# Both parts of an activation in one 512-wide product, and the farthest tap of the feed-forward convolution on ScalarE

## The chip, the cores and the metric

The kernel runs on one core of a Trainium2 chip. The metric is the time of one execution on the device in microseconds; the time shown is the median of three runs. TensorE (PE) multiplies matrices, VectorE (DVE) and ScalarE (ACT) work elementwise, each engine takes its instructions in the order in which they are written for it, and an instruction may have to wait for semaphores that other engines raise. PE writes its sums to PSUM; everything else lies in SBUF.

## The reference, cut to what matters

Two layers over x of 256 positions by 1024 channels. A layer is a norm, a projection into three mixers (SSD, retention, gated linear attention), their merge and a residual add; then a norm and a feed-forward part with a causal convolution of three taps over positions, and a residual add. A last norm ends it. All in float32.

```python
def conv_ffn(h, w_up, conv_w, conv_b, w_down):
    u = causal_dwconv(h @ w_up, conv_w, conv_b)      # 1024 -> 2 x 2816 channels, 3 taps
    gate, val = jnp.split(u, 2, axis=-1)
    return (jax.nn.silu(gate) * val) @ w_down        # 2816 -> 1024
...
    xbc = jax.nn.silu(causal_dwconv(xbc, ssm_conv_w, ssm_conv_b))   # 768 channels, 4 taps
...
for i in range(DEPTH):
    h = rms_norm(x, norm_mix_g[i])
    x = x + hybrid_mixer(h, w_in[i], ...)
    h = rms_norm(x, norm_ffn_g[i])
    x = x + conv_ffn(h, w_up[i], ffn_conv_w[i], ffn_conv_b[i], w_down[i])
return rms_norm(x, norm_f_g)
```

## The kernel before

Each float32 product is made from three products of a rounded type (fp32r). An operand is split into a high part and a low part (what the rounding left): high times high, high times low, low times high are added up in PSUM. The weights come from HBM in pieces of 128x1024 (tile raw). ACT casts a piece to its high part (whi, L183) and DVE subtracts that to get the low part (wlo, L184): each piece costs one such cast and one such subtraction, in the order in which the pieces are used. The activations are split once per norm into the tiles slot_h and slot_l (L302 on ACT, L303 on DVE).

There are two forms of product. In the form tok (tok_major, L274 to L276) the activations are the stationary operand and the weights stream 512 wide; a result takes two PSUM banks. In the form chan (chan_steps, L227 to L229) the weights are stationary and the activations stream, 256 positions wide, so that the result has channels on the partitions, as the convolutions need them. One chan result holds two channel blocks of 128 side by side in one PSUM bank (128x512) and takes 16 groups of three products: 8 steps k over the 1024 input channels for each of the two blocks j. A layer has 9 chan results in its mixers (xbc 3, rq 2, rk 2, gq 1, gk 1) and 22 in its feed-forward part (up), 62 in all.

The scale of the norm is not in the operands: it is applied when a result leaves PSUM, by a multiply with r_bc, the factors of the 256 positions on all partitions. DVE works them out (a chain of small steps that ends with dg, L319), PE spreads them (L322) and ACT copies them out of PSUM (L324). Until then no result can be drained.

PSUM has eight banks: four for the tag mm, which the chan and tok results share, and four for the tag mx.

The start of a mixer: xbc blocks 2 and 0 are made at once, in steps that alternate (chan_two, by the list LATE = (0, 2, 8, 10, 4, 12, 6, 14), in which 0 to 6 are block 2 and 8 to 14 block 0); then xbc block 1, then a narrow result (narrow, L256 and L260, one bank, drained by L475 into the tile small), then z in the form tok. Each xbc result goes through take_xbc: multiply by r_bc (L459), two activations for the nearest tap and the bias (L463), six steps for the other taps on DVE (L466), a tanh (L470), a last step (L471).

The feed-forward part alternates: block j of up (16 chan groups) and the down products of an earlier block (12 products 512 wide, L1024 to L1026, in mx). activate() drains an up block: multiply by r_bc (L1007), two activations (L1012), four steps for the two other taps (L1014), silu (L1016), gate times value (L1017), and the split into high and low part (L1018 on ACT, L1019 on DVE). Layer 0's down is followed by the residual adds (L365) and by layer 1's start.

The order on each engine is fixed when the program is built, by a scheduler that goes over what the generators yield.

## Time and profile before

| | |
|---|---|
| median of 3 runs | 933.4 us (932.29 to 935.02) |
| the profiled execution | 932.3 us, its span 930.5 us |
| mean granted clock of PE | 0.994 |
| busy: PE / weight loads | 914.5 / 816.1 us |
| busy: DVE / ACT / POOL | 712.9 / 506.8 / 78.4 us |
| HBM read | 165.81 MB, 179 GB/s over the span |

A busy time is the sum of an engine's instructions as the profiler saw them. Instructions on PE overlap, so the length of one is more than the time from its start to the next one's start; it is that distance that tells what a product costs. The granted clock is that of PE, as a share of its full 2.4 GHz.

### The profile page before, as it was taken

The page shows a single profiled execution, that of the slowest core. Times are in us where ns is not written, and L with a number is a line of the kernel's source. Part 1 is how long each engine was busy: PE and PEld are TensorE (multiplying, and loading weights), DVE is VectorE, ACT ScalarE, POOL GpSimd, SP SyncE. Part 2 cuts the span into 40 slices and gives each one's busy share as a digit, 9 for nine tenths or more (in the row PEclk, how much of TensorE's full clock was granted, in tenths as well). Part 3 has the DMA queues.
Part 4 walks back from the last instruction along what each step waited for, and adds up shares of the span by engine and source line. Part 5 has one row for each costly group of instructions (what it writes and reads, how often), then busy time and mean ns, then how long its engine had stood idle before and what let it go on. Part 6 is the DMA issues. An engine that isn't in the chain of part 4 may idle for free.

```text
span 930.5 us, 14996 instructions
## 1 busy us (share of the span) xinstructions
PE 914.5 (98%) x5726; PEld 816.1 (88%) x5726; DVE 712.9 (77%) x1111; ACT 506.8 (54%) x748; POOL 78.4 (8%) x74
## 2 busy tenths in 40 slices
PE   8999999999999999999999999999999999999995
PEld 7879889888889999999898898888888999999994
DVE  6976888576768887787799578777667697777775
ACT  6765454454456555555566635554545575555552
POOL 3032200003200000000002131000120000000001
PEclk9999999999999999999999999999999999999998
DMA  7775655556655656555466556444665566555531
GB/s 255 276 243 166 219 172 170 152 162 210 201 181 161 202 183 186 188 192 181 147 186 183 198 168 218 158 139 156 206 212 194 169 188 189 190 183 184 183 109 46
DMA packets 51288, 169.94 MB, mean 183 GB/s; under 512 B 5968, under 2 KB 8336, under 8 KB 51088
## 3 DMA queue, kind: packets, MB, share of 16 engines
q1 hardware_dynamic: 50928, 168.46, 56.3%
q8 instruction: 45, 0.74, 0.3%
q10 hardware_dynamic: 288, 0.52, 0.2%
q14 instruction: 27, 0.22, 0.1%
HBM read 165.81 MB, written 1.05 MB: 179 GB/s over the span
## 4 chain that ended last, share of the span: by engine, by line
PE 94%; DVE 3%; ACT 1%; DMA 1%; issue 0%; SPq 0%; ACTq 0%
PE mm L227 13%; PE mm L228 13%; PE mm L229 13%; PE mm L274 12%; PE mm L275 12%; PE mm L276 12%; PE mx L1025 4%; PE mx L1024 4%; PE mx L1026 4%; PE mx L555 2%; DVE wlo L184 1%; PE mx L558 1%; DVE xbc L466 1%; PE mx L542 1%; DMA x_t<-x_t 1%; PE mx L726 1%
## 5 line engine op out<-in xcount | busy, mean ns | idle before, releaser
L184 DVE TENSOR_TENSOR wlo<-raw,whi 128x1024 fp32r<-128x1024 f32 (+1 forms) x300 | 377.6, 1261 | 123.6 <-ACT whi L183 120.6
L183 ACT CAST whi<-raw 128x1024 fp32r<-128x1024 f32 (+1 forms) x302 | 311.7, 1034 | 266.4 <-PE mm L276 109.3
L227 PE MATMUL mm<-slot_h,whi 128*128 128x256 f32 x992 | 282.4, 285 | 2.2 <-ACT slot_h L302 2.2
L228 PE MATMUL mm<-slot_l,whi 128*128 128x256 f32 x992 | 281.5, 284 | 0.1
L229 PE MATMUL mm<-slot_h,wlo 128*128 128x256 f32 x992 | 281.5, 284 | 0.0
L274 PE MATMUL mm<-whi,slot_h 128*128 128x512 f32 x512 | 203.9, 398 | 0.0
L275 PE MATMUL mm<-wlo,slot_h 128*128 128x512 f32 x512 | 200.4, 391 | 0.0
L276 PE MATMUL mm<-whi,slot_l 128*128 128x512 f32 x512 | 200.3, 391 | 0.0
L227 PEld LDWEIGHTS mm<-slot_h,whi 128*128 128x128 f32 x992 | 190.5, 192 | 4.9 <-ACT slot_h L302 2.6
L228 PEld LDWEIGHTS mm<-slot_l,whi 128*128 128x128 f32 x992 | 190.7, 192 | 2.1 <-DVE slot_l L303 0.3
L229 PEld LDWEIGHTS mm<-slot_h,wlo 128*128 128x128 f32 x992 | 190.7, 192 | 0.1
L274 PEld LDWEIGHTS mm<-whi,slot_h 128*128 128x128 f32 x512 | 96.2, 188 | 20.6 <-issue 0.7
L276 PEld LDWEIGHTS mm<-whi,slot_l 128*128 128x128 f32 x512 | 96.1, 188 | 20.3
L275 PEld LDWEIGHTS mm<-wlo,slot_h 128*128 128x128 f32 x512 | 96.3, 188 | 18.7
L1014 DVE SCALAR_TENSOR_TENSOR tm<-tm,par 128x255 f32<-128x255 f32 (+1 forms) x176 | 73.6, 478 | 0.7 <-ACT tm L1012 0.7
L1024 PE MATMUL mx<-whi,slot_h 128*128 128x512 f32 x176 | 69.1, 392 | 0.0
L1025 PE MATMUL mx<-wlo,slot_h 128*128 128x512 f32 x176 | 69.0, 392 | 0.0
L1026 PE MATMUL mx<-whi,slot_l 128*128 128x512 f32 x176 | 68.5, 389 | 0.0
L1012 ACT ACTIVATE tm<-tm,par 128x256 f32<-128x256 f32 x88 | 48.0, 592 | 4.3 <-DVE tm L1007 4.3
L1007 DVE TENSOR_TENSOR tm<-mm,r_bc 128x512 f32<-128x512 f32 x44 | 30.4, 690 | 23.1 <-PE mm L229 23.1
L1018 ACT CAST slot_h<-tm 128x256 fp32r<-128x256 f32 x44 | 17.9, 406 | 49.1 <-DVE tm L1017 49.0
L1026 PEld LDWEIGHTS mx<-whi,slot_l 128*128 128x128 f32 x176 | 33.1, 188 | 7.1
(193 smaller groups left out, 758.6 us busy)
## 6 DMA issues: line engine op xcount, KB each, us to landing
raw<-w_all SPq DMA_DIRECT2D x292, 512.0 KB, 3.5
gate_b<-gate_b SPq DMA_DIRECT2D x12, 256.0 KB, 3.5
st<-ret_decay SPq DMA_DIRECT2D x8, 384.0 KB, 3.8
raw<-w_all SPq DMA_DIRECT2D x10, 256.0 KB, 3.9
x_t<-x_t SPq DMA_DIRECT2D x4, 256.0 KB, 5.8
xt<-x_tok SPq DMA_DIRECT2D x1, 1024.0 KB, 6.3
r_c<-q SPq DMA_DIRECT2D x16, 64.0 KB, 2.0
r_d<-q SPq DMA_DIRECT2D x16, 64.0 KB, 2.0
```

What stands on the lines that cost most here:

```text
L183: nc.scalar.copy(h_out, r_in)
L184: nc.vector.tensor_tensor(l_out, r_in, h_out.bitcast(F32), ALU.subtract)
L227: nc.tensor.matmul(o, lhsT=wh[:, c], rhs=ah[:, k, :], start=first, stop=False)
L228: nc.tensor.matmul(o, lhsT=wh[:, c], rhs=al[:, k, :], start=False, stop=False)
L229: nc.tensor.matmul(o, lhsT=wl[:, c], rhs=ah[:, k, :], start=False, stop=last)
L274: nc.tensor.matmul(acc[t], lhsT=ah[:, k, c], rhs=wh, start=first, stop=False)
L275: nc.tensor.matmul(acc[t], lhsT=ah[:, k, c], rhs=wl, start=False, stop=False)
L276: nc.tensor.matmul(acc[t], lhsT=al[:, k, c], rhs=wh, start=False, stop=last)
L1014: nc.vector.scalar_tensor_tensor(a[:, d:], u[:, :T - d], mx.pc("fconv_w", 3 * ct + 2 - d), a[:, d:], ALU.mult, ALU.add)
L1024: nc.tensor.matmul(o, lhsT=ah[:, a, tok], rhs=wh, start=first, stop=False)
L1025: nc.tensor.matmul(o, lhsT=ah[:, a, tok], rhs=wl, start=False, stop=False)
L1026: nc.tensor.matmul(o, lhsT=al[:, a, tok], rhs=wh, start=False, stop=last)
```

## The change

The high and the low part of an activation now lie side by side in one tile (both, 128 x n x 2 x 256). In a chan group the high part of the weights is multiplied with both at once, 512 wide, and the low part of the weights with the high part, 256 wide, into the first half. A chan result is then two halves that have to be added: it takes two PSUM banks (a pair), and a new function joined() copies the second half out on ACT and adds the first to it on DVE, into an SBUF tile. The multiply by r_bc works in place on that tile. The four banks of mm become two pairs; a tok result takes one pair, as its two banks did; narrow takes a pair and uses half of one bank.

In the feed-forward convolution the farthest tap of each of the two channel blocks becomes an ACT activation into a tile far, and one DVE add of 128x2x254 adds it for both; two of the four steps on DVE go.

```diff
--- before.py
+++ after.py
@@ -156,9 +156,8 @@
 
     slots = []
     for i, n in enumerate((KT, KT, 4)):
-        h = cpool.tile([P, n, T], F32R, name=f"slot_h{i}")
-        lo = cpool.tile([P, n, T], F32R, name=f"slot_l{i}")
-        slots.append((h, lo))
+        both = cpool.tile([P, n, 2, T], F32R, name=f"slot{i}")
+        slots.append((both[:, :, 0, :], both[:, :, 1, :], both))
 
 
     loaded = {}
@@ -193,7 +192,7 @@
         return (a[:, c] for a in piece(p + o // step))
 
     def mm_tile():
-        return ps.tile([P, 512], F32, name="mm", tag="mm", bufs=4)
+        return ps.tile([P, 2, 512], F32, name="mm", tag="mm", bufs=2)
 
     def mx_tile():
         return ps.tile([P, 512], F32, name="mx", tag="mx", bufs=4)
@@ -214,27 +213,31 @@
         return r_bc.unsqueeze(1).to_broadcast([P, 2, T])
 
 
-    def chan_steps(l, kind, idx, act, acc, ks, nk=KT, cols=256, width=256, col0=0):
-
-        ah, al = act
-        nj = width // P
+    def chan_steps(l, kind, idx, act, acc, ks, nk=KT):
+
+
+        ah, _, both = act
         for k in ks:
-            wh, wl = weight(l, kind, idx, k, cols)
-            for j in range(nj):
-                c = slice(col0 + j * P, col0 + (j + 1) * P)
-                o = acc[:, j * T:(j + 1) * T]
-                first, last = k == 0 and j == 0, k == nk - 1 and j == nj - 1
-                nc.tensor.matmul(o, lhsT=wh[:, c], rhs=ah[:, k, :], start=first, stop=False)
-                nc.tensor.matmul(o, lhsT=wh[:, c], rhs=al[:, k, :], start=False, stop=False)
-                nc.tensor.matmul(o, lhsT=wl[:, c], rhs=ah[:, k, :], start=False, stop=last)
-
-    def chan_major(l, kind, idx, act, nk=KT, **more):
+            wh, wl = weight(l, kind, idx, k, 256)
+            for j in range(2):
+                c = slice(j * P, (j + 1) * P)
+                nc.tensor.matmul(acc[:, j, :], lhsT=wh[:, c], rhs=both[:, k], start=(k == 0), stop=False)
+                nc.tensor.matmul(acc[:, j, :T], lhsT=wl[:, c], rhs=ah[:, k, :], start=False, stop=(k == nk - 1))
+
+    def joined(acc):
+
+        u = t_main()
+        nc.scalar.copy(two(u), acc[:, :, T:])
+        nc.vector.tensor_tensor(two(u), acc[:, :, :T], two(u), ALU.add)
+        return u
+
+    def chan_major(l, kind, idx, act, nk=KT):
         acc = mm_tile()
         for k in range(0, nk, 2):
-            chan_steps(l, kind, idx, act, acc, (k, k + 1), nk, **more)
+            chan_steps(l, kind, idx, act, acc, (k, k + 1), nk)
             if k < nk - 2:
                 yield
-        return acc
+        return joined(acc)
 
     def chan_two(l, kind, idx, act, take):
 
@@ -243,13 +246,13 @@
             i, k = n // 8, n % 8
             chan_steps(l, kind, idx[i], act, acc[i], (k, k + 1))
             if k == KT - 2:
-                take(idx[i], acc[i])
+                take(idx[i], joined(acc[i]))
             yield
 
     def narrow(l, act):
 
-        ah, al = act
-        acc = mm_tile()
+        ah, al, _ = act
+        acc = mm_tile()[:, 0, :]
         both = piece(PIECE_AT[l, "small", 0][0])[0].rearrange("p (k c) -> p k c", c=P)
         for k in range(KT):
             def low():
@@ -264,8 +267,9 @@
 
     def tok_major(l, kind, act, chunk=0, nk=KT):
 
-        ah, al = act
-        acc = [mm_tile() for _ in range(2)]
+        ah, al, _ = act
+        pair = mm_tile()
+        acc = [pair[:, t, :] for t in range(2)]
         for k in range(nk):
             wh, wl = weight(l, kind, chunk + k // 4, k % 4, 512)
             for t in range(2):
@@ -444,8 +448,7 @@
             nc.gpsimd.memset(self.wa, 0.0)
             for o in (32, 96):
                 nc.sync.dma_start(self.wa[o:o + 16, :], wa2[l])
-            y_h, y_l = slots[1]
-            self.y_dst = [(y_h[:, 0:4, :], y_l[:, 0:4, :]), (y_h[:, 4:8, :], y_l[:, 4:8, :]), slots[2]]
+            self.y_dst = [tuple(a[:, o:o + 4] for a in slots[1]) for o in (0, 4)] + [slots[2]]
 
         def pc(self, name, i=0, n=1):
             return self.pr[:, PO[name] + i:PO[name] + i + n]
@@ -455,7 +458,7 @@
             half = self.half
             if not hasattr(self, "xbc"):
                 self.xbc = mix.tile([P, 6, T], F32, name="xbc", tag="g_work")
-            ub = t_main()
+            ub = acc
             nc.vector.tensor_tensor(two(ub), two(acc), bc2(self.norm.r_bc), ALU.mult)
             for j in range(2):
                 ct = 2 * b + j
...
@@ -999,20 +1002,22 @@
 
 
         fx = slots[1]
-        ah, al = slots[2]
+        ah, al, _ = slots[2]
         dacc = []
 
         def activate(j, acc):
-            ub = t_main()
+            ub = acc
             nc.vector.tensor_tensor(two(ub), two(acc), bc2(norm.r_bc), ALU.mult)
             cv = t_main()
+            far = tmp.tile([P, 512], F32, name="far", tag="gt", bufs=4)
             for i in range(2):
                 ct = j + NF * i
-                u, a = ub[:, i * T:(i + 1) * T], cv[:, i * T:(i + 1) * T]
+                u, a, f = (q[:, i * T:(i + 1) * T] for q in (ub, cv, far))
                 nc.scalar.activation(a, u, AF.Identity, scale=mx.pc("fconv_w", 3 * ct + 2), bias=mx.pc("fconv_b", ct))
-                for d in (1, 2):
-                    nc.vector.scalar_tensor_tensor(a[:, d:], u[:, :T - d], mx.pc("fconv_w", 3 * ct + 2 - d),
-                                                   a[:, d:], ALU.mult, ALU.add)
+                nc.scalar.activation(f, u, AF.Copy, scale=mx.pc("fconv_w", 3 * ct))
+                nc.vector.scalar_tensor_tensor(a[:, 1:], u[:, :T - 1], mx.pc("fconv_w", 3 * ct + 1), a[:, 1:],
+                                               ALU.mult, ALU.add)
+            nc.vector.tensor_tensor(two(cv)[:, :, 2:], two(cv)[:, :, 2:], two(far)[:, :, :T - 2], ALU.add)
             nc.scalar.activation(cv[:, :T], cv[:, :T], AF.Silu)
             nc.vector.tensor_tensor(cv[:, :T], cv[:, :T], cv[:, T:], ALU.mult)
             nc.scalar.copy(ah[:, j % 4, :], cv[:, :T])
```

The part left out gives operands of the same shapes their new layout. What the change does to the order shows at three places. First PE at the start of layer 0's mixer, from the end of xbc block 1 (mm_378 before, mm_347 now) through narrow (L260 before, L263 now) to z (L274 before, L278 now). Before:

```order
L227 MATMUL mm_378<-slot_h0_87,whi_228 128x256
L228 MATMUL mm_378<-slot_l0_88,whi_228 128x256
L229 MATMUL mm_378<-slot_h0_87,wlo_229 128x256
L260 MATMUL mm_452<-slot_h0_87,whi_246 128x256 [waits Activation_49]
L256 MATMUL mm_452<-slot_l0_88,whi_246 64x256
...
L274 MATMUL mm_477<-whi_278,slot_h0_87 128x512
L275 MATMUL mm_477<-wlo_279,slot_h0_87 128x512
```

And of the change:

```order
L326 MATMUL mx_301<-dg_298,ones_79 128x256 [waits DVE_49]
L225 MATMUL mm_347<-slot0_87,wlo_218 128x256
L224 MATMUL mm_347<-slot0_87,whi_217 128x512
L225 MATMUL mm_347<-slot0_87,wlo_218 128x256
L263 MATMUL mm_407<-slot0_87,whi_231 128x256 [waits DVE_49,PE_49]
L259 MATMUL mm_407<-slot0_87,whi_231 64x256
...
L278 MATMUL mm_432<-whi_255,slot0_87 128x512 [waits DVE_49]
L279 MATMUL mm_432<-wlo_256,slot0_87 128x512
```

A group is two products in place of three. The first products of narrow and of z now wait for DVE: by the semaphores' values, narrow for the join of xbc block 0 (tm_332), z for the multiply into small.

Second, DVE at the same start, from dg to small. Before (tm_334 and tm_365 are xbc blocks 2 and 0):

```order
L319 TENSOR_SCALAR dg_326<-cs_76,rs_y_311 128x128
L184 TENSOR_TENSOR wlo_279<-raw_277,whi_278 128x1024 [waits DMAHW4_49,Activation_49]
L459 TENSOR_TENSOR tm_334<-mm_168,r_bc_331 128x512 [waits Activation_49]
L184 TENSOR_TENSOR wlo_349<-raw_347,whi_348 128x1024 [waits DMAHW5_49,Activation_49]
...
L184 TENSOR_TENSOR wlo_381<-raw_379,whi_380 128x1024 [waits DMAHW7_49,Activation_49]
L471 SCALAR_TENSOR_TENSOR xbc_333<-tm_344,xbc_333 128x512 [waits Activation_49]
L459 TENSOR_TENSOR tm_365<-mm_169,r_bc_331 128x512 [waits PE_49]
...
L475 TENSOR_TENSOR small_475<-mm_452,r_bc_331 128x256 [waits PE_49]
```

Of the change (tm_276 and tm_332 are the same two blocks, and L231 is the join):

```order
L231 TENSOR_TENSOR tm_276<-mm_165,tm_276 128x512 [waits Activation_49]
...
L183 TENSOR_TENSOR wlo_256<-raw_254,whi_255 128x1024 [waits DMAHW4_49,Activation_49]
...
L323 TENSOR_SCALAR dg_298<-cs_76,rs_y_283 128x128
L183 TENSOR_TENSOR wlo_320<-raw_318,whi_319 128x1024 [waits DMAHW5_49,Activation_49]
L462 TENSOR_TENSOR tm_276<-tm_276,r_bc_303 128x512 [waits Activation_49]
L183 TENSOR_TENSOR wlo_350<-raw_348,whi_349 128x1024 [waits DMAHW7_49,Activation_49]
...
L474 SCALAR_TENSOR_TENSOR xbc_305<-tm_315,xbc_305 128x512 [waits Activation_49]
L231 TENSOR_TENSOR tm_332<-mm_166,tm_332 128x512 [waits Activation_49]
L183 TENSOR_TENSOR wlo_410<-raw_408,whi_409 128x1024 [waits DMAHW1_49,PE_49]
L462 TENSOR_TENSOR tm_332<-tm_332,r_bc_303 128x512 [waits DVE_49]
...
L478 TENSOR_TENSOR small_430<-mm_407,r_bc_303 128x256 [waits PE_49]
```

The join of block 2 and one more wlo stand ahead of dg. The join of block 0 stands behind the whole convolution of block 2, and small behind the multiply, the join and five of the six steps of block 0 (one after the other in the rows left out, with a multiply of r_a between).

Third, DVE in the feed-forward part, one block in the steady state. Before:

```order
L1007 TENSOR_TENSOR tm_8458<-mm_8397,r_bc_7439 128x512 [waits PE_49]
L184 TENSOR_TENSOR wlo_8473<-raw_8471,whi_8472 128x1024 [waits DMAHW7_49,Activation_49]
L1014 SCALAR_TENSOR_TENSOR tm_8460<-tm_8458,par1_75,tm_8460 128x255 [waits Activation_49] x2
```

Of the change:

```order
L231 TENSOR_TENSOR tm_8233<-mm_8188,tm_8233 128x512 [waits Activation_49]
L1010 TENSOR_TENSOR tm_8233<-tm_8233,r_bc_6870 128x512 [waits DVE_49]
L183 TENSOR_TENSOR wlo_8271<-raw_8269,whi_8270 128x1024 [waits DMAHW2_49,Activation_49]
L1018 SCALAR_TENSOR_TENSOR tm_8237<-tm_8233,par1_75,tm_8237 128x255 [waits Activation_49] x2
L1020 TENSOR_TENSOR tm_8237<-tm_8237,far_8238 128x2x254 [waits DVE_49,Activation_49]
```

The multiply waited for PE; now the join does, by way of ACT's copy. The weight pieces keep their places between the steps, and the added far tap comes where two steps of a tap stood.

## Rows read from the trace of the kernel before

**Rows 1.** The page, busy time of each engine (share of the span) and instructions.
```profile
PE 914.5 (98%) x5726; PEld 816.1 (88%) x5726; DVE 712.9 (77%) x1111; ACT 506.8 (54%) x748; POOL 78.4 (8%) x74
```

**Rows 2.** The page, the chain that ended last, by engine.
```profile
PE 94%; DVE 3%; ACT 1%; DMA 1%; issue 0%; SPq 0%; ACTq 0%
```

**Rows 3.** Timeline of PE, 256-wide products: start, us, engine, line, operation, times.
```profile
601.15 0.28 PE L227 MATMUL mm<-slot_h,whi 128*128 128x256 f32 x1
...
601.51 0.28 PE L227 MATMUL mm<-slot_h,whi 128*128 128x256 f32 x1
```

**Rows 4.** Timeline of PE, 512-wide products.
```profile
610.00 0.39 PE L274 MATMUL mm<-whi,slot_h 128*128 128x512 f32 x1
...
610.68 0.39 PE L274 MATMUL mm<-whi,slot_h 128*128 128x512 f32 x1
```

**Rows 5.** Windows: length, busy of PE, PEld, DVE, ACT, POOL, granted clock, DMA.
```profile
8.00:11.40 3.40, 3.40 (x16) 3.40 (x17) 3.19 (x7) 3.40 (x9) 0.00 (x0) 0.50 0.91 327
...
26.00:45.00 19.00, 19.00 (x103) 15.96 (x102) 18.59 (x34) 14.36 (x21) 0.00 (x0) 1.00 0.77 280
477.00:497.00 20.00, 20.00 (x128) 18.10 (x127) 19.58 (x34) 13.48 (x19) 0.00 (x0) 1.00 0.50 162
751.00:900.00 149.00, 149.00 (x1057) 140.56 (x1057) 119.94 (x183) 84.92 (x126) 0.00 (x0) 1.00 0.58 184
```

**Rows 6.** Timeline of ACT in the feed-forward part; in brackets the idle time before.
```profile
805.99 1.05 ACT L183 CAST whi<-raw 128x1024 fp32r<-128x1024 f32 x1 [1.60 <-PE mm L228]
806.94 1.09 ACT L1012 ACTIVATE tm<-tm,par 128x256 f32<-128x256 f32 x2
...
814.49 1.05 ACT L183 CAST whi<-raw 128x1024 fp32r<-128x1024 f32 x1 [1.60 <-PE mm L228]
```

**Rows 7.** The page, costliest groups: count, busy us, mean ns, idle before.
```profile
L227 PE MATMUL mm<-slot_h,whi 128*128 128x256 f32 x992 | 282.4, 285 | 2.2 <-ACT slot_h L302 2.2
```

**Rows 8.** Groups by line, a copy out of PSUM on ACT.
```profile
L590 ACT COPY sg_c<-mx 128x512 f32<-128x512 f32 x4 | 2.3, 580 | 0.0
```

**Rows 9.** Timeline of DVE at the start of layer 0's mixer.
```profile
24.44 0.48 DVE L319 TENSOR_SCALAR dg<-cs,rs_y 128x128 f32<-128x128 f32 x2
...
28.30 2.45 DVE L466 SCALAR_TENSOR_TENSOR xbc<-tm,half,xbc 128x255 f32<-128x255 f32 x6
30.67 1.22 DVE L184 TENSOR_TENSOR wlo<-raw,whi 128x1024 fp32r<-128x1024 f32 x1
31.80 0.68 DVE L471 SCALAR_TENSOR_TENSOR xbc<-tm,xbc 128x512 f32<-128x512 f32 x1
32.40 0.68 DVE L459 TENSOR_TENSOR tm<-mm,r_bc 128x512 f32<-128x512 f32 x1
...
37.64 0.41 DVE L475 TENSOR_TENSOR small<-mm,r_bc 128x256 f32<-128x256 f32 x1
```

**Rows 10.** Timeline of DVE in the feed-forward part, the four steps of the taps.
```profile
808.21 1.67 DVE L1014 SCALAR_TENSOR_TENSOR tm<-tm,par 128x255 f32<-128x255 f32 x4
```

**Rows 11.** Timeline of ACT at the start of layer 0's mixer.
```profile
25.80 0.37 ACT L324 COPY r_bc<-mx 128x256 f32<-128x256 f32 x1 [1.73 <-PE mx L322]
```

**Rows 12.** Timeline of PE there: narrow's first product and z's.
```profile
27.52 0.28 PE L260 MATMUL mm<-slot_h,whi 128*128 128x256 f32 x1
...
29.38 0.40 PE L274 MATMUL mm<-whi,slot_h 128*128 128x512 f32 x1
```

**Rows 13.** Timeline of DVE and PE at the start of layer 1.
```profile
460.73 1.37 DVE L365 TENSOR_TENSOR xt<-xt,mx 128x512 f32<-128x512 f32 x2 [1.22 <-PE mx L1026]
...
464.86 0.28 PE L227 MATMUL mm<-slot_h,whi 128*128 128x256 f32 x1
...
485.70 0.40 PE L274 MATMUL mm<-whi,slot_h 128*128 128x512 f32 x1
```

**Rows 14.** Timeline of PE, two of its pauses in layer 0.
```profile
7.40 0.38 PE L227 MATMUL mm<-slot_h,whi 128*128 128x256 f32 x1 [2.16 <-ACT slot_h L302]
...
55.03 0.39 PE L593 MATMUL mx<-da,cs 128*128 128x8 f32 x2 [0.84 <-DVE da L584]
```

More of the change, by code (lines that the diff above doesn't have):

```diff
@@ L527, in turn @@
                         nc.tensor.transpose(pt[:, j * T + t * P:j * T + (t + 1) * P], self.merged[t][:, c:c + P], ident)
-                mh, ml = (a[:, 2 * q:2 * q + 2, :].rearrange("p k t -> p (k t)") for a in slots[0])
-                nc.scalar.activation(mh, pt, AF.Copy, scale=0.5)
-                nc.vector.scalar_tensor_tensor(ml, pt, 0.5, mh.bitcast(F32), ALU.mult, ALU.subtract)
+                mh, ml = (a[:, 2 * q:2 * q + 2, :] for a in slots[0][:2])
+                nc.scalar.activation(mh, two(pt), AF.Copy, scale=0.5)
+                nc.vector.scalar_tensor_tensor(ml, two(pt), 0.5, mh.bitcast(F32), ALU.mult, ALU.subtract)
                 yield 1
         def branch_operand(self, y, g, dst):
-            h, lo = dst
+            h, lo, _ = dst
             for c2 in range(2):
```

## The prediction

> **What bounds the kernel now.** I read the shares of busy time first: TensorE (PE) is busy 98% of the span [rows 1], and the chain that ended last is 94% PE and 3% DVE [rows 2]. So time moves only with PE's own work and with its few pauses. Then the timeline of single products. In the products that the change touches, one group of three 256-wide products starts every 0.36 us, 0.120 us a product [rows 3]; three 512-wide ones take 0.68, 0.227 each [rows 4]. Twice the columns therefore cost 0.107 us more, and each product carries 0.0133 us that does not grow with its width. Last the windows by stage. In the feed-forward part (FFN) PE is busy all 149 of 149 us and DVE 119.94, ACT 84.92; at both mixer starts DVE is busy 18.59 of 19.00 and 19.58 of 20.00 us while PE never stops [rows 5]. There DVE is full already, only nothing makes PE wait for it. The FFN period is 8.50 us [rows 6], which is 48 products by 0.120 and 12 by 0.227 (8.48): PE's own time, with ACT waiting 1.60 us of it for PE.
>
> **The products.** The page counts 992 products on the first of the group's three lines [rows 7], so 992 groups. A group goes from 3 x 0.120 = 0.360 to 0.227 + 0.120 = 0.347. That is 0.0133 us each, 13.2 us in all: the same 768 columns pass, and one fixed part is saved. Of these groups 704 (44 blocks of 16) are in the FFN, 288 in the mixers. The rows of the two widths bound the saving between 0.013 and 0.014.
> The Trainium skill, page "TensorE: Matmul & The Clock Gate", section "Back-to-back issue gap", puts an isolated product at its columns by 2.4 GHz plus 2.5 ns. By that a group would save 2.5 ns and all of them 2.5 us. The rows here show 0.120 us at 256 columns where that formula gives 0.109, so the trace disagrees and I go by the rows.
>
> **Joining.** Each of the 62 accumulators now needs an ACT copy out of PSUM and a DVE add. The copy: 580 ns, by a PSUM copy of the same 128x512 [rows 8]. The add: 0.68 us long by the DVE steps of the same shape, and 0.60 us apart back to back (31.80 to 32.40 [rows 9]). The multiply by r_bc stays, but now reads what the join wrote.
>
> **The farthest tap.** Of four DVE steps of a block, 1.67 us together [rows 10], two go (0.8 us); one add of 0.60 comes. ACT gets two activations at 0.50 (two take 1.09 [rows 6]). Per FFN block: DVE has 119.94/149 x 8.50 = 6.84 us and goes to 6.84 - 0.80 + 0.60 + 0.60 = 7.24. ACT has 84.92/149 x 8.50 = 4.84 and goes to 4.84 + 0.58 + 1.0 = 6.4. PE's period becomes 16 x 0.347 + 12 x 0.227 = 8.27. Both stay below it, and the order interleaves the weight casts with the block's chain, so FFN stays PE's and gains 0.213 us a block, 9.4 us of the 13.2. If that cover of about 1 us on DVE were gone, each 0.1 us beyond 8.27 would cost 4.4 us.
>
> **The PSUM pairs.** Four single banks become two pairs. What was "PE may run three accumulators ahead of the drain" becomes one. In the mixer start the accumulators come as xbc2, xbc0, xbc1, narrow, z. By the order, narrow's first product waits for the join of xbc0 and z's first waits for the multiply that reads narrow (small). Before, z's first product waited for no drain. Both drains stand deep in the queue of the full DVE, behind the normalization, the casts' second halves (wlo) and the convolution of xbc2, all of which run in order.
>
> Layer 0, on DVE, by its order and the rows [rows 9]. The scales dg end at 24.92 before (24.44 + 0.48). Now one join (0.60) and one more wlo (1.13, 30.67 to 31.80) stand ahead: 26.65. From dg's end to the end of r_bc were 1.25 us (25.80 + 0.37 [rows 11]): r_bc at 27.9. Multiply 0.60, to 28.55. The next wlo waits for a cast that follows r_bc on ACT (1.05): 29.05 to 30.2. Six convolution steps 2.37 (28.30 to 30.67), to 32.6; wlo to 33.7; the tanh step 0.60, to 34.3; **the join of xbc0 to about 34.95**. Only now narrow may start, which began at 27.52 [rows 12]. It takes 1.86 us, to 36.8. DVE goes on: wlo (36.1), multiply (36.7), r_a (37.3), five convolution steps (39.3), small (0.41): 39.7. So **z starts at 39.7 in place of 29.38, +10.3 us**. PE's pauses within are first some 2 us for dg, which is late, then about 7, then about 3.
>
> Layer 1 the same way. Products start at 464.86 [rows 13]. The four adds of the residual (the first two 1.37 us from 460.73 [rows 13]) now have two wlo between them and end near 465.4; the order puts all transposes and the first split behind them, so products start at 467.0. 32 groups by 0.347 and the r_bc products (0.6): both accumulators done at about 478.5. xbc2 is done one step of eight earlier, 477; then a cast 1.05, wlo 1.13 and the join 0.60: xbc1 starts at 479.7, ends 485.3. On DVE follow the wlo of that last part (cast 1.05, wlo 1.13), the tanh step and the join of xbc0: 488.6. Then multiply, five convolution steps (2.0) and small, near 491.9: **z at 491.9 in place of 485.70, +6.2 us**.
>
> **Small terms.** The clock: in the stretch 8.00 to 11.40, after PE had been idle 2.16 us, the granted clock is 0.50, the lower of its two levels, with PE busy throughout [rows 5, 14]. Work worth 1.7 us at full clock is lost there. After the pauses of 7 and 3 us I charge that once, 1.7 (bounds 0 and 3.4). What z's delay gives back: PE's wait of 0.84 us for the state decay at 54.19 to 55.03 [rows 14] should vanish, with small others near it: -1.0. FFN starts and last blocks: the last block's chain is longer by copy, join and one add less the taps, 1 us, of which the 27 down products that lie ahead of its first use by the order (27 x 0.227 = 6.1 us) leave some 0.25 a layer: +0.5.
>
> **Sum.** 896 groups outside the two starts: -11.9. Layer 0 +10.3, layer 1 +6.2 (their own 96 groups are in these), clock +1.7, returned -1.0, FFN edges +0.5: +5.8. Against the profiled execution's own 932.3 us that is 938.1; the median of the runs, 933.4, lies 1.1 above it, so **939 us**.
>
> Bounds. The starts: with each of my ACT waits and gaps removed from DVE's chain, layer 0 loses 1 us and layer 1 2 us; with narrow at the half clock and casts released late by the pauses both grow by 2 to 3. Clock 0 to 3.4. Together 934 to 946 around the forecast.
>
> **Rivals.**
> 1. The drains come in time and PE never pauses: then only the saving is left, 933.4 - 13.2 = 920. For it: in the FFN the same two pairs suffice, as a drain has 8.27 us there. Against it: DVE full at both starts [rows 5] and the places of the joins in its order. It is faster than before as soon as the two starts cost under about 8 us together, in place of 16.5; about 933 if they cost 11. The point that decides is whether DVE has the join of xbc0 done by 27 us or by 35.
> 2. ACT and DVE become the FFN's bound. A block's chain is now copy, join, multiply, activations, taps, add, silu, product, split, all in strict order with three casts and three wlo. If their loop takes 9.0 us where I add up 7.24 of work, the FFN costs 44 x 0.73 = 32 us more: about 971. For it: the loop has two more handovers between ACT and DVE than before. Against it: each engine keeps over 1 us of slack in a period, and the casts are not all behind the chain.
> 3. The wide product saves next to nothing. Then the starts stand alone: 933.4 + 16.5 + 1.7 - 0.5 = 951, less whatever small saving is left. Against it: both widths stand in the rows at full rate. By the formula of the Trainium skill's page named above, 2.5 us would be saved: an estimate of about 949.
>
> **Chances.** A measurement of this kernel can't tell less than about 0.3% from no change, so 930.6 to 936.2 counts as the same. The forecast (936 to 947) 0.59; starts that are hidden by about half (930.6 to 936) 0.15; rival 1 and what lies near it, below 930.6, 0.20; rivals 2 and 3, 0.03 each. So faster 0.20, same 0.15, slower 0.65. The range reaches from 927, midway to rival 1, which leaves some 0.14 of it out, up to 948, which leaves 0.06 out; the forecast by itself is 934 to 946.
>
> **What would show it.** Right: groups of 0.347 us; an FFN period near 8.27 with DVE and ACT still waiting for PE; PE idle for several us in front of narrow and of z, released by the join and by small, at about 35 and 39.7 us and about 488.6 and 491.9; z later by 10 and 6 us. Wrong: z within 3 us of its old place, an FFN period above 8.4, or groups still at 0.36. Most likely to be wrong is the length of the two pauses, which rests on my walk down DVE's queue.

## The result, and the profile after

The changed kernel takes 961.6 us (median of 4 runs, 958.46 to 964.41) against 932.9 us before: the ratio is 1.030, with a 95% interval of 1.0264 to 1.0341. It is slower, as forecast, but by 28.7 us in place of 5.8.

The first lines of the page after, as in [rows 1, 2, 7]: busy time, then the chain that ended last, then the group of the wide products (busy, mean ns, idle time before them and what ended most of it).

```profile
PE 919.8 (96%) x4734; PEld 769.3 (80%) x4734; DVE 750.1 (78%) x1129; ACT 574.8 (60%) x898; POOL 76.7 (8%) x74
...
PE 86%; DVE 7%; ACT 2%; DMA 2%; issue 1%; SPq 1%; POOL 0%; DVEq 0%; ACTq 0%; POOLq 0%
...
L224 PE MATMUL mm<-slot,whi 128*128 128x512 f32 x992 | 354.7, 400 | 6.9 <-DVE tm L231 4.5
```

PE was 94% of the chain and is 86%; DVE went from 3% to 7%. What PE waits for is in the view of waits (total us, times, longest). Before, it held 4.1 us in three rows; it now has 29.5, of which these:

```profile
PE mm L263 <- DVE tm L231: 11.2, 2, 7.6
PE mx L545 <- DVE tx L565: 5.7, 2, 2.9
PE mm L224 <- DVE tm L231: 4.5, 3, 1.5
PE mm L278 <- DVE small L478: 2.8, 2, 1.6
PE mm L224 <- DVE slot L307: 2.4, 3, 1.3
```

The first, third and fourth are drains of PSUM pairs: narrow, the products after two open pairs, z. The second is not a drain at all, and nothing in the forecast answers to it. The fifth stands at the very start of layer 0, where PE had waited 2.2 us for the same splits on ACT before [rows 7].

Where the span's 30.5 us (930.5 to 961.0) came in, by the first product of each stage, or of its last group, on PE's timeline:

| stretch | before | after | more by | forecast |
|---|---|---|---|---|
| layer 0, start to z | to 29.38 | to 39.76 | +10.4 | +10.3 |
| layer 1, last group of down products to z | 464.16 to 485.70 | 477.63 to 508.92 | +9.8 | +6.2 |
| z to the first up product, layer 0 | 29.38 to 275.69 | 39.76 to 290.44 | +4.4 | with the next |
| the same, layer 1 | 485.70 to 730.58 | 508.92 to 761.53 | +7.7 | -3.6 for both |
| up and down, both layers | 188.47, 187.55 | 187.19, 186.99 | -1.8 | -8.9 |

The forecast's column puts 192 groups (-2.6) and the returned wait (-1.0) into the mixers and 704 groups (-9.4) and the edges (+0.5) into the FFN; its 1.7 for the clock had no place.

Layer 0's start went by the walk down DVE's queue, at its end almost to the digit. DVE there, with the join of xbc block 0 behind the tanh step of block 2 (start us, length, line, operation):

```profile
28.01 0.68 DVE L462 TENSOR_TENSOR tm<-tm,r_bc 128x512 f32<-128x512 f32 x1
28.85 1.23 DVE L183 TENSOR_TENSOR wlo<-raw,whi 128x1024 fp32r<-128x1024 f32 x1 [0.16 <-ACT whi L182]
30.00 2.45 DVE L469 SCALAR_TENSOR_TENSOR xbc<-tm,half,xbc 128x255 f32<-128x255 f32 x6
32.36 1.22 DVE L183 TENSOR_TENSOR wlo<-raw,whi 128x1024 fp32r<-128x1024 f32 x1
33.50 0.68 DVE L474 SCALAR_TENSOR_TENSOR xbc<-tm,xbc 128x512 f32<-128x512 f32 x1
34.10 0.68 DVE L231 TENSOR_TENSOR tm<-mm,tm 128x512 f32<-128x512 f32 x1
```

and PE's timeline there and in layer 1, where in [rows 12, 13] narrow and z follow without a pause:

```profile
34.93 0.55 PE L263 MATMUL mm<-slot,whi 128*128 128x256 f32 x1 [7.64 <-DVE tm L231]
...
39.76 0.50 PE L278 MATMUL mm<-whi,slot 128*128 128x512 f32 x1 [1.27 <-DVE small L478]
...
504.58 0.35 PE L263 MATMUL mm<-slot,whi 128*128 128x256 f32 x1 [3.61 <-DVE tm L231]
508.92 0.80 PE L278 MATMUL mm<-whi,slot 128*128 128x512 f32 x1 [1.56 <-DVE small L478]
```

The clock behind the pauses: windows with the length, then PE's busy time first, DVE's third and the granted clock after POOL's.

```profile
27.00:35.00 8.00, 0.36 (x3) 0.10 (x1) 7.84 (x13) 5.31 (x8) 0.00 (x0) 0.77 0.93 322
35.00:38.40 3.40, 3.40 (x16) 3.28 (x16) 3.30 (x6) 1.09 (x2) 0.00 (x0) 0.54 0.97 388
...
126.90:133.70 6.80, 6.80 (x21) 5.17 (x20) 3.97 (x8) 1.81 (x4) 0.00 (x0) 0.50 0.46 154
...
304.50:308.00 3.50, 3.46 (x19) 3.05 (x20) 2.42 (x4) 1.74 (x4) 0.00 (x0) 1.00 0.77 235
...
509.00:512.50 3.50, 3.50 (x9) 2.73 (x9) 2.89 (x4) 0.73 (x2) 0.00 (x0) 0.50 0.42 142
...
597.90:604.70 6.80, 6.80 (x22) 5.19 (x20) 4.00 (x8) 1.81 (x4) 0.00 (x0) 0.50 0.46 155
```

The first shows both sides of the pause: DVE 98% busy, PE 5%. Behind the pauses in front of narrow (7.64 us), the SSD result (2.77 in layer 0, 2.93 in layer 1) and z of layer 1 (3.61 and 1.56) PE has no gap and runs at or near the lower of its two levels. Behind the single pause of 1.50 us at the first feed-forward start (304.50) the clock stays at 1.00.

The wide products: PE's timeline in a steady FFN block, and two multiplies of consecutive blocks on DVE.

```profile
352.06 0.39 PE L224 MATMUL mm<-slot,whi 128*128 128x512 f32 x1
352.29 0.28 PE L225 MATMUL mm<-slot,wlo 128*128 128x256 f32 x1
352.40 0.40 PE L224 MATMUL mm<-slot,whi 128*128 128x512 f32 x1
...
353.46 0.40 PE L224 MATMUL mm<-slot,whi 128*128 128x512 f32 x1
...
361.06 0.69 DVE L1010 TENSOR_TENSOR tm<-tm,r_bc 128x512 f32<-128x512 f32 x1
...
369.45 0.70 DVE L1010 TENSOR_TENSOR tm<-tm,r_bc 128x512 f32<-128x512 f32 x1
```

Four groups take 1.40 us, 0.35 each. Over all 990 recorded pairs the median is 0.235 us from a wide product to the narrow one and 0.117 back: 0.352. The period is 8.39.

A check on the whole: I sorted the distances between the starts of PE's products by kind of pair and took the median of each kind as its price. What exceeds it by more than 0.35 us at once is 3.7 us before and 31.2 after (+27.5, the pauses); what exceeds it by less is 20.7 and 29.7 (+9.0, mostly the clock behind them). The rest of the span's +30.5 is -6.0, which I put down to the cheaper products.

### The profile page after: what moved, and what is told of

Read it like the earlier page. It is cut to its first block, busy times and chain, and to the rows that moved or that the text cites. A ratio compares the mean times of both kernels' runs of the same rounds, so it can differ in the third digit from the quotient of the medians.

```text
span 961.0 us, 13129 instructions
## 1 busy us (share of the span) xinstructions
PE 919.8 (96%) x4734; PEld 769.3 (80%) x4734; DVE 750.1 (78%) x1129; ACT 574.8 (60%) x898; POOL 76.7 (8%) x74
## 4 chain that ended last, share of the span: by engine, by line
PE 86%; DVE 7%; ACT 2%; DMA 2%; issue 1%; SPq 1%; POOL 0%; DVEq 0%; ACTq 0%; POOLq 0%
PE mm L224 23%; PE mm L278 12%; PE mm L225 11%; PE mm L280 11%; PE mm L279 11%; PE mx L1029 4%; PE mx L1030 4%; PE mx L1031 4%; DVE wlo L183 2%; DMA raw<-w_all 1%; PE mx L558 1%; ACT whi L182 1%; PE mx L545 1%; DVE xbc L469 1%; PE mx L729 1%
## 5 line engine op out<-in xcount | busy, mean ns | idle before, releaser
L224 PE MATMUL mm<-slot,whi 128*128 128x512 f32 x992 | 354.7, 400 | 6.9 <-DVE tm L231 4.5
L225 PE MATMUL mm<-slot,wlo 128*128 128x256 f32 x992 | 278.5, 281 | 0.0
L224 PEld LDWEIGHTS mm<-slot,whi 128*128 128x128 f32 x992 | 186.3, 188 | 53.5 <-DVE tm L231 5.7
L278 PE MATMUL mm<-whi,slot 128*128 128x512 f32 x512 | 206.8, 404 | 2.8 <-DVE small L478 2.8
L280 PE MATMUL mm<-whi,slot 128*128 128x512 f32 x512 | 202.4, 395 | 0.0
L279 PE MATMUL mm<-wlo,slot 128*128 128x512 f32 x512 | 202.2, 395 | 0.0
L225 PEld LDWEIGHTS mm<-slot,wlo 128*128 128x128 f32 x992 | 187.7, 189 | 2.3 <-DVE wlo L183 0.5
L278 PEld LDWEIGHTS mm<-whi,slot 128*128 128x128 f32 x512 | 97.7, 191 | 24.5 <-DVE small L478 3.3
L280 PEld LDWEIGHTS mm<-whi,slot 128*128 128x128 f32 x512 | 97.4, 190 | 21.0
L279 PEld LDWEIGHTS mm<-wlo,slot 128*128 128x128 f32 x512 | 97.9, 191 | 19.1
L1029 PE MATMUL mx<-whi,slot 128*128 128x512 f32 x176 | 69.3, 394 | 0.3 <-ACT slot L1023 0.3
L1030 PE MATMUL mx<-wlo,slot 128*128 128x512 f32 x176 | 69.0, 392 | 0.0
L1031 PE MATMUL mx<-whi,slot 128*128 128x512 f32 x176 | 68.4, 390 | 0.0
L231 DVE TENSOR_TENSOR tm<-mm,tm 128x512 f32<-128x512 f32 x62 | 42.4, 683 | 0.7 <-ACT tm L230 0.5
```

The lines of the kernel that those rows point to most:

```text
L224: nc.tensor.matmul(acc[:, j, :], lhsT=wh[:, c], rhs=both[:, k], start=(k == 0), stop=False)
L225: nc.tensor.matmul(acc[:, j, :T], lhsT=wl[:, c], rhs=ah[:, k, :], start=False, stop=(k == nk - 1))
L278: nc.tensor.matmul(acc[t], lhsT=ah[:, k, c], rhs=wh, start=first, stop=False)
L279: nc.tensor.matmul(acc[t], lhsT=ah[:, k, c], rhs=wl, start=False, stop=False)
L280: nc.tensor.matmul(acc[t], lhsT=al[:, k, c], rhs=wh, start=False, stop=last)
L1029: nc.tensor.matmul(o, lhsT=ah[:, a, tok], rhs=wh, start=first, stop=False)
```

## The experiments

All are compared with the kernel before on the same chip; its median was 932.9 to 934.5 us.

**The far tap alone.** The kernel before with the new taps:

```diff
+            far = tmp.tile([P, 512], F32, name="far", tag="gt", bufs=4)
...
-                for d in (1, 2):
...
+                nc.scalar.activation(f, u, AF.Copy, scale=mx.pc("fconv_w", 3 * ct))
...
+            nc.vector.tensor_tensor(two(cv)[:, :, 2:], two(cv)[:, :, 2:], two(far)[:, :, :T - 2], ALU.add)
```

> The kernel before with only the farthest tap moved to ScalarE (two activations and one add in place of two DVE steps a block); products and PSUM as before. Theory Q (the added time comes from PE waiting for drains that stand deep in DVE's queue at a few places, and from the low clock behind these pauses): PE sets the period of the feed-forward part, so 933 us, within 2. Rival W (the added elementwise work on ACT and DVE is what costs): ACT gets 1.0 us a block, so 935 to 940.

933.3 us, ratio 0.9997 (0.9982 to 1.0012). It costs and gives nothing that can be told from none.

**The rest of the change without the far tap.** The four DVE steps come back, all else stays.

> The changed kernel with the old taps (four DVE steps a block, no far tile); 512-wide products, pairs and joins stay. Theory Q: the pauses stand at the mixers, which this doesn't touch, so 958 to 964 as the changed kernel. Rival W: if the far tap's extra activations cost, 950 to 956.

961.8 us, 1.0305 (1.0273 to 1.0337), as the changed kernel. The far tap plays no part.

**Narrow without a pair.**

```diff
-        acc = mm_tile()[:, 0, :]
+        acc = mx_tile()
```

> The changed kernel with the narrow result in a bank of the tag mx, so that it takes no pair; z then takes the pair of xbc block 0. Theory Q: narrow follows xbc block 1 with no wait and z waits only for the join of xbc block 0, near 35 us in place of 39.8 in layer 0 and some 4 us earlier in layer 1; with less of the low clock behind it 948 to 954. Rival W: the work is the same, so 958 to 964.

954.6 us, 1.0236 (1.0206 to 1.0265): just outside theory Q's range of 948 to 954, and far from rival W's. z waits for the join, at the time at which narrow had waited:

```profile
35.10 0.77 PE L278 MATMUL mm<-whi,slot 128*128 128x512 f32 x1 [5.20 <-DVE tm L231]
```

**Joins first.** The kernel of the last experiment, with both joins ahead of both convolutions:

```diff
             if k == KT - 2:
-                take(idx[i], joined(acc[i]))
+                done.append((idx[i], joined(acc[i])))
+                if kind == "up" or len(done) == 2:
+                    for a in done:
+                        take(*a)
+                    done = []
```

> The changed kernel, narrow in a bank of mx, with both joins of the first two xbc blocks ahead of the convolutions of both in the program (the work is the same, only its order differs). Theory Q (the place of the joins in DVE's queue makes PE wait): z waits for neither drain, the 7.3 us of that wait and some 3 us at the low clock go from 954.6: 942 to 947. Rival W (the work counts, not its place): 952 to 956.

949.5 us, 1.0159 (1.0132 to 1.0185). z follows xbc block 1 at once, with the same instructions in another order:

```profile
27.09 0.28 PE L225 MATMUL mm<-slot,wlo 128*128 128x256 f32 x1
27.20 0.39 PE L283 MATMUL mm<-whi,slot 128*128 128x512 f32 x1
...
57.49 0.36 PE L601 MATMUL mx<-da,cs 128*128 128x8 f32 x2 [1.70 <-DVE da L592]
```

So the place of the joins makes PE wait there, which shows theory Q for this pause. But the time fell by 5.1 us and not by 8 to 12: both numeric ranges miss. In layer 0 nothing at all was gained. z starts at 27.20 in place of 35.10, but the first up product comes at 286.56 in both runs. PE, now early, catches up with DVE: it waits 0.93 us at 41.78 and 1.70 in the last row above, which was 0.84 in [rows 14]. And the clock falls behind the later pauses, to 0.50 in

```profile
58.40:61.80 3.40, 3.40 (x10) 2.48 (x10) 3.40 (x6) 0.90 (x1) 1.91 (x1) 0.50 0.61 219
119.80:130.00 10.20, 9.68 (x27) 6.90 (x28) 6.02 (x10) 1.80 (x4) 0.00 (x0) 0.50 0.30 103
```

The mean granted clock is 0.985 before this edit and with it. What was gained came in layer 1, most of it at its start.

**No join.** `joined` returns the first half, which the multiply reads from PSUM; the product of the high weights with the low activations is left out of the results of all 62 chan accumulators.

> The changed kernel without the joins: the multiply by r_bc reads the first half straight from PSUM and the second half (high weights by low activations) is left out of the results; products, pairs and the far tap stay. Theory Q (two pairs, whose drain lies behind DVE's queue): narrow still waits, now for the multiply of xbc block 0, some 5 us in layer 0 and 2 in layer 1, the wait in front of the transposes of the SSD result goes: 940 to 948. Rival W (the work of the joins is what costs): 925 to 930.

945.1 us, 1.0115 (1.0100 to 1.0130). The work of the joins is gone, and the kernel is still 11 us slower than before. Its largest waits are for the multiplies of pairs, and for dg, which these multiplies need:

```profile
PE mm L277 <- DVE tm L461: 4.1, 1, 4.1
PE mx L325 <- DVE dg L322: 3.5, 1, 3.5
...
PE mm L226 <- DVE tm L461: 2.6, 1, 2.6
PE mm L277 <- DVE small L477: 2.1, 1, 2.1
...
PE mx L544 <- DVE tx L564: 0.5, 1, 0.5
```

That refutes rival W as the only cause. The time is inside theory Q's range, but the places are not those expected: narrow waits only 0.8 us, and xbc block 1 and z wait instead. The wait in front of the SSD result (the last row) falls from 5.7 to 0.5.

**rq and rk in the old form.**

```diff
+                if kind in ("rq", "rk"):
+                    o = acc[:, 0, j * T:(j + 1) * T]
...
+                    nc.tensor.matmul(o, lhsT=wh[:, c], rhs=ah[:, k, :], start=first, stop=False)
+                    nc.tensor.matmul(o, lhsT=wh[:, c], rhs=al[:, k, :], start=False, stop=False)
+                    nc.tensor.matmul(o, lhsT=wl[:, c], rhs=ah[:, k, :], start=False, stop=last)
...
-        return joined(acc)
+        return acc[:, 0, :] if kind in ("rq", "rk") else joined(acc)
```

> The changed kernel with rq and rk (8 of the 62 results) made of three 256-wide products in half a pair, without join. Theory Q: the waits of PE for the SSD result's last step on DVE (2.9 us in each layer, with some 2.5 us at the lower clock behind each) come from DVE being late by these joins, and go: 950 to 953. Rival S (the scheduler's new order puts the transposes there in any case): 960 to 963.

951.7 us, 1.0196 (1.0170 to 1.0223): inside theory Q's range, 9.9 us for 8 accumulators. PE's wait for the SSD result falls from 5.7 us to

```profile
PE mx L552 <- DVE tx L572: 0.2, 1, 0.2
```

In the profiled execution the mixers behind z take 3.8 and 5.1 us less than in the changed kernel, 8.8 together (41.27 to 288.21 and 507.08 to 754.62). That is more than half of the 15.7 us by which they missed the forecast (12.1 more in place of 3.6 less).

**Wide products in the FFN alone.** A first form took its banks by turns from one PSUM tile of four banks:

```diff
+    banks = ps.tile([P, 4, 512], F32, name="mm", tag="mm", bufs=1)
```

> Wide products, joins and pairs in the feed-forward part alone; the mixers with three 256-wide products and single banks as before (one PSUM tile of four banks from which both take their banks in turn). Theory Q: the mixers go back to the times of before, the feed-forward part keeps what the changed kernel has there (1.3 and 0.6 us less than before), so 929 to 933. Rival W: the joins and the far tap cost in the feed-forward part, 936 or more. Rival T (the wide product saves nothing): 933 to 936.

1043.2 us, 1.118 (1.116 to 1.120): it tests none of the theories. PE waits for drains of other banks of that tile, in the mixers too:

```profile
PE mm L232 <- DVE tm L478: 10.0, 4, 4.5
PE mm L294 <- DVE gt L531: 8.8, 6, 1.5
PE mm L240 <- DVE tm L247: 8.7, 4, 2.9
```

The second form gives each channel block its own tile of one bank, out of four as before:

```diff
-        return ps.tile([P, 2, 512], F32, name="mm", tag="mm", bufs=2)
+        return ps.tile([P, 512], F32, name="mm", tag="mm", bufs=4)
...
+        return [mm_tile(), mm_tile()] if kind == "up" else mm_tile()
...
+        for j, a in enumerate(acc):
+            o = u[:, j * T:(j + 1) * T]
+            nc.scalar.copy(o, a[:, T:])
+            nc.vector.tensor_tensor(o, a[:, :T], o, ALU.add)
```

> Wide products in the feed-forward part alone, each channel block's accumulator in a bank of its own out of four single banks (the join is two copies and two adds of 128x256); the mixers in the form of before with the banks of before. It does with separate PSUM tiles what the one tile of four banks did not. Theory Q: mixers as before, feed-forward part 0.6 to 1.3 us a layer faster, 928 to 933. Rival W (joins and far tap cost by their work): above 935. Rival T (wide product saves nothing): 933 to 936.

933.1 us, 0.9986 (0.9975 to 0.9996). With the mixers in the form of before, single banks included, 28 us of the loss are gone: all of it lies in the mixers. The FFN keeps its 44 joins and far taps and is no slower for them. The gain is at the edge of what can be told from none.

**Wide products first.** The same, with another order of four products:

```diff
                 for j in range(2):
                     c = slice(j * P, (j + 1) * P)
                     nc.tensor.matmul(acc[j], lhsT=wh[:, c], rhs=both[:, k], start=(k == 0), stop=False)
+                for j in range(2):
+                    c = slice(j * P, (j + 1) * P)
                     nc.tensor.matmul(acc[j][:, :T], lhsT=wl[:, c], rhs=ah[:, k, :], start=False, stop=(k == nk - 1))
```

> The same, with the two wide products of a step k ahead of the two 256-wide ones (wide, wide, narrow, narrow in place of wide, narrow twice). In the changed kernel a wide product takes 0.235 us when a 256-wide one follows and a tok product of the same width 0.227. Theory V (the 8 ns belong to the change of width): one change in place of two, 16 groups lose 0.06 us a block, 1 to 3 us faster than the kernel without this order. Rival: the 8 ns belong to the wide product's own operand or output; no difference.

928.8 us, 0.9947 (0.9928 to 0.9967), 4.3 us less than without this order. Theory V's sign is right and its size too small. Its reason is not borne out: a wide product behind which another wide one follows still takes 0.233 us. Two groups on PE:

```profile
352.60 0.62 PE L225 MATMUL mm<-slot,whi 128*128 128x512 f32 x2
353.05 0.40 PE L228 MATMUL mm<-slot,wlo 128*128 128x256 f32 x2
353.28 0.63 PE L225 MATMUL mm<-slot,whi 128*128 128x512 f32 x2
```

The FFN period is 8.29 us, 0.10 less than in the changed kernel, near the 8.27 forecast.

**The operand as one run.** The streamed operand of that kernel written as 512 in place of 2 by 256.

> The kernel with wide products in the feed-forward part alone and the wide ones first, with the wide product's streamed operand written as one run of 512 elements in place of 2 by 256 (the same bytes). There a wide product takes 0.233 us, a tok product 0.227. Theory A (the two-part operand costs the 6 ns): 704 products give 4 us, so 924 to 926. Rival: the operand is merged anyway and nothing changes, 928 to 930.

928.5 us, 0.9947 (0.9929 to 0.9964), the period 8.29: nothing. The traces of both runs, and of the changed kernel, give the operand of every wide product as one run of 512 elements. So the edit left the instruction as it was, and theory A falls by its premise: there was no operand in two parts.

**The first two up blocks in the old form**, so that the third finds two free banks:

```diff
-            if kind == "up":
+            if kind == "up" and idx > 1:
```

> The same kernel (not flat) with the first two blocks of the feed-forward part in the old form, one bank each, so that the third block finds two free banks. Theory Q: PE's wait of 1.1 us for the first block's join in each layer goes, and some of the low clock behind it; the 64 groups lose 0.7 us: 924 to 928. Rival (the wait is hidden elsewhere): 928 to 931.

926.8 us, 0.9918 (0.9900 to 0.9936). The wait for the first join is gone. This is the lowest median here, 0.8% under the kernel before.

**Both of the last two edits together.**

> Both edits of the two kernels ahead of it. If both theories hold, 920 to 924; if only the start counts, 924 to 928; if neither, 928 to 931.

927.9 us, 0.9934 (0.9911 to 0.9957): as with the start alone.

## Why the prediction was wrong in size

**Right.** The bound and its loss: PE waits at both starts for drains that stand deep in DVE's queue. In layer 0 narrow began at 34.93 (forecast 34.95) and z at 39.76 (39.7). The far tap is free. ACT and DVE do not become the FFN's bound. On the way two things came out otherwise, and did not show in z's time. dg was done at 26.06 in place of 26.65, so that PE never paused for it (forecast: some 2 us), and DVE then waited for casts. And narrow, at the low clock, took 3.6 us in place of 1.86, which only shortened PE's next pause to 1.27 us (forecast: about 3), since z had to wait for DVE in any case.

**The step that failed** is the sum's first term, "896 groups outside the two starts: -11.9". I walked DVE's queue to z and took all behind it as pure saving; the bounds, too, widen only the starts and the clock. The mixers behind z lost 12.1 us where that term and the returned wait made it 3.6 less. The returned wait itself came out: the 0.84 us of [rows 14] are gone from the view of waits. Of the 24.7 us by which the span missed the forecast, these mixers are 15.7, the FFN 7.1 and layer 1's start 3.6, less the 1.7 charged for the clock. The largest part is one wait of PE, twice: the transposes of the SSD result, which in [rows 1, 2] no row hints at because they came in time. DVE and POOL in layer 0:

```profile
106.06 1.23 DVE L183 TENSOR_TENSOR wlo<-raw,whi 128x1024 fp32r<-128x1024 f32 x1 [1.45 <-ACT whi L182]
107.20 0.68 DVE L231 TENSOR_TENSOR tm<-mm,tm 128x512 f32<-128x512 f32 x1
107.92 0.69 DVE L701 TENSOR_TENSOR s<-tm,r_a 128x512 f32<-128x512 f32 x1
...
122.63 1.93 POOL L715 TENSOR_TENSOR r_b<-r_b,mean 128x1024 f32<-128x1024 f32 x1 [10.29 <-DVE rs_y L293]
122.83 1.75 DVE L292 SCALAR_TENSOR_TENSOR rs_a<-rs_a,rs_v 128x4 f32<-128x4 f32 x1
124.81 1.29 DVE L565 TENSOR_TENSOR tx<-tx,rs_y 128x512 f32<-128x512 f32 x2
...
125.55 0.44 PE L545 MATMUL mx<-cs,tx 128*128 128x128 f32 x2 [2.77 <-DVE tx L565]
```

rk's last product ended at 105.05. Its second half has to be copied (ACT, 0.58 us), the join stands behind a wlo that waits for a cast, and the first step that uses it starts at 107.92, 2.9 us after the products; before, it started 0.04 us after them (96.56, 96.60). A further 1.6 us go into a step of 128x4 elements that takes 1.75 us in place of 0.16: POOL's subtraction runs at the same time. In the kernel before that subtraction started at 112.30, when tx was done (110.78 to 112.06); the new order of DVE puts the reduction that releases it ahead of tx's last steps. Behind the wait of 2.77 us the granted clock is 0.50 for 6.8 us with PE busy throughout (the window above), which loses another 3.4. Layer 1 has the same: 2.93 us, and 6.8 at 0.50. With 1.8 for the 3.7 us at 0.50 behind z of layer 1, and less the 0.84 returned and 1.5 for 192 groups that are 0.008 us shorter, that makes some 12 us, an estimate from these rows, of the 12.1 measured.

The runs without the eight joins of rq and rk and without any join show the wait all but gone. How the 2.77 divide between the lag and the collision with POOL was read from the rows, not tested; without the eight joins the collision goes as well, as POOL's subtraction there starts behind the last step of tx, at 125.70.

The Trainium skill, page "SBUF — State Buffer", section "SBUF: two separate sides", says that VectorE and GpSimd share one pair of ports as an exclusive lock, which whichever starts first holds for its whole instruction, and that a VectorE instruction with two inputs in SBUF needs the pair when GpSimd reads SBUF. The rows agree: the step of 1.75 us has two such inputs and ends at 124.58, POOL's 1.93 us at 124.56; in layer 1 it is 1.91 beside 1.90 (both from 593.50).

**The price of a group** was mis-sized: 0.352 at the median in place of 0.347. That is 7.9 us for 992 groups, and -6.0 in the balance, in place of -13.2. I took the wide product's 0.227 from products that follow others of their width. Between narrow ones it takes 0.235.

**FFN.** The period came out at 8.39 in place of 8.27, for the most part for that reason. And "FFN edges +0.5" missed a wait of 1.5 us in each layer for the join of the first block, since the third up block needs that pair. With 704 groups at 0.005 more than forecast these two waits make some 6.5 of the FFN's 7.1. The run with the first two blocks in the old form has no such wait, and is 2.0 us faster than the one with 2.2 us of it; its expectation spoke of low clock behind it as well, which the row at 304.50 does not show.

**Layer 1's start** has the forecast's waits (1.5 for xbc block 1, 3.6 for narrow, 1.6 for z) and 3.5 us more. Counted from the last group of down products, xbc block 1 starts 2.0 us later than forecast, narrow 2.5, z 3.5. The residual adds ahead of it (1.1 us of waits) are the first part. The last part stands in front of small:

```profile
505.83 2.70 DVE L469 SCALAR_TENSOR_TENSOR xbc<-tm,half,xbc 128x255 f32<-128x255 f32 x6 [0.67 <-ACT xbc L466]
508.44 0.42 DVE L478 TENSOR_TENSOR small<-mm,r_bc 128x256 f32<-128x256 f32 x1
```

DVE waits 0.67 us for ACT there and then has six steps ahead of small, where the forecast had no wait and five. What lies between is not resolved.

**The clock** cost up to 9.0 us by the balance, not 1.7: I charged one pause. The granted clock says the same: in its four low stretches PE was busy for 21.9 us at 0.50, before in one for 3.4 (the last 10 us of either kernel left out), and half of the difference is 9.3. Some of it is hidden, as narrow ran at the low clock in both layers and z then waited for DVE. The long pauses have low clock behind them, narrow's in layer 0, the SSD result's in both layers and the pair in layer 1; behind the single ones of 1.5 us there is none.

**Rivals.** The drains did not come in time (rival 1), ACT and DVE did not bind (rival 2). Rival 3, little saved by the wide product, was half true.

## What to carry to other kernels

Before you merge accumulators into wider ones, count how many PE may have open, and follow the queue of the engine that drains them to the end of every stage, not only through the first place where it binds: here a drain of rk that was 2.9 us late made PE wait for another result some 18 us on, far behind z. Charge the longer pauses of PE with the slow clock behind them, which here came to as much as a third on top of all pauses. Where only one stage profits, change that stage: the wide product pays in the FFN (0.8% with the wide ones side by side and a start in the old form) and the kernel loses 3% where the mixers use it as well.

## What the runs showed of the hardware that was not expected

A 512-wide product between 256-wide ones takes 0.235 us to the next start, with 0.117 back; two wide and two narrow ones in turn have medians of 0.233, 0.231, 0.115 and 0.119, which is 0.698 for two groups in place of 0.704. By the FFN period the gain is larger still, 0.10 us a block for 8 such turns. That the order is the cause is shown; why is open. The form of the operand is not it, since it was one run of 512 elements throughout.

The clock answered to pauses, but not by their length alone: behind 2.77, 7.64 and 3.61 with 1.56 us the granted clock was 0.50, 0.54 and 0.50 with PE busy throughout, behind a single 1.50 us it was 1.00. In the run with wide products in the FFN alone and a tile for each bank (933.1 us) two pauses of the same 1.56 us differ:

```profile
56.30:59.70 3.40, 3.40 (x11) 2.49 (x10) 2.19 (x4) 1.73 (x3) 0.45 (x1) 0.51 0.56 164
297.00:300.40 3.40, 3.39 (x19) 3.00 (x20) 3.06 (x6) 3.10 (x6) 0.00 (x0) 1.00 0.44 149
```

The first pause ended at 54.82, and PE went on with six products of 8 columns before its wide ones; the second ended at 297.01, and wide products followed at once. What makes the difference was not tested.

One PSUM tile of four banks, used by turns, made PE wait for readers of banks that it did not write (1043 us); four tiles of one bank, taken by turns as well, did not (933 us). The two also differ in the join, which is one copy and one add there and two of each here. These are waits for semaphores that the program sets; that PSUM itself asks for them is not shown.
